# Expert layer of a transformer block: GpSimd left with transfers alone, weights written in sixteen pieces, selection in 16-bit one-hot form, list work in finer pieces

## The chip, the cores and the metric

One core of a Trainium2 chip runs the whole kernel in one launch. The metric is the time of an execution in microseconds on the device; the number for a kernel is the median of three runs.

## What is computed

One layer of a backbone for 512 latent and 256 context tokens of width 1024: a projection, a bidirectional mLSTM, grouped-query attention, a first layer norm, and then PEER, a layer that picks 128 of 16384 experts for every token. The change is in the last part:

```python
def _peer(h, wq, keys, u, v):          # P_BLOCK 128 tokens, 8 heads, 128 keys per half, top 16
    def block(xt):
        q = (xt @ wq).reshape(P_BLOCK, P_HEADS, 2, P_HALF)
        s = jnp.einsum('nhpd,hpkd->nhpk', q, keys)
        s1, i1 = lax.top_k(s[:, :, 0], P_TOPK)
        s2, i2 = lax.top_k(s[:, :, 1], P_TOPK)
        cand_s = (s1[..., :, None] + s2[..., None, :]).reshape(P_BLOCK, P_HEADS, P_TOPK * P_TOPK)
        cand_i = (i1[..., :, None] * N_KEYS + i2[..., None, :]).reshape(P_BLOCK, P_HEADS, P_TOPK * P_TOPK)
        top_s, pos = lax.top_k(cand_s, P_TOPK)
        idx = jnp.take_along_axis(cand_i, pos, axis=-1).reshape(P_BLOCK, P_HEADS * P_TOPK)
        g = jax.nn.softmax(top_s, axis=-1).reshape(P_BLOCK, P_HEADS * P_TOPK)
        act = jax.nn.gelu(jnp.einsum('nd,ned->ne', xt, u[idx]), approximate=False)
        return jnp.einsum('ne,ned->nd', g * act, v[idx])
```

and x = LN(alpha * x + gate2 * PEER(...)) behind it.

## The kernel before

The 512 tokens go in four tiles of 128. Each tile passes three stages.

**Selection** (`select`) is work of VectorE on a scratch that lies in the big tile `work` (128 x 16384 f32): top 16 of each of 16 score rows (L896 to L900), sums of candidates (L970, L973), top 16 of those. `weigh` then turns the positions into the two expert indices and a weight per pick, `iig`. For each half q, VectorE compares positions with 0 to 15 (is_equal, L952), GpSimd multiplies that one-hot tile by the indices (L954), and VectorE reduces (L962). The scores of tiles 1 to 3 come back from memory as `scfx` and `scfy`; those of tile 1 are read by GpSimd's queue.

**Lists** (`prelude`): transposes of `iig` (ptr, L991), then 16 units of 8 tokens. VectorE builds one-hot tiles A (L1008) and B (L1011), TensorE multiplies them into pf (which experts are used, and whether by one token) and pW (L1021), and ScalarE puts pW into `work` as the matrix of weights by expert and token. That matrix, Wd, 8.4 MB, goes to memory in four writes (L1028, SyncE's queue). `tables` and `look_up` (small steps that pass between TensorE, VectorE and ScalarE: pft, ppr, ppo, ppk) number the used experts and give two lists: `ri`, the expert of each of 29 x 128 rows, and `wi`, its row in Wd.

**Blocks** (`blocks`): 29 blocks of 128 experts per tile. GpSimd gathers uv (both matrices' rows, 1 MB) and wr (the weights, 64 KB) by the lists (L1108). In 12 of the 29 blocks every expert has one token: `token` finds it from wr on VectorE (jt, ti, L1147 and L1148), GpSimd gathers that token's row xg (512 KB), and VectorE takes the dot with u (L1168). In the other 17, TensorE transposes u (put, L1268; copied to ut by ScalarE, L1269) and multiplies by all tokens (s, L1282). Gelu on ScalarE (L1283), a multiply by wr on VectorE (L1284; for one-token blocks on ScalarE, L1185), and TensorE adds the block to py (L1196). `finish` adds the residual and does the second layer norm, two of its steps on GpSimd (L1255, L1258).

**Order.** A step of `blocks` issues for block i+5 the gathers (stage r of PIPE), for i+4 jt and ti (k), for i+3 the xg (u), for i+1 the dot (d), for i+2 the transposes (o), and so on to py of block i (a). The lists of tile t+1 are made while the blocks of tile t run: the driver (L1323 on) lets `select` and `prelude` go on by one step (one `yield`) whenever a table of costs (C_SEL, C_OH, ...; 43 steps and 131 units per tile) says so, at most to five blocks ahead of the tile's end (LATE). HEADS gives the steps of tile 0's selection and lists between which a step of the scores of tiles 2 and 3 is done (pwq, psc). `order_of` mixes the 12 one-token blocks into the 29. A scheduler then sets the order of each engine's instructions by dependences and the order in which the code issued them; each engine, and each DMA queue that it issues to, goes through them in order.

## Time and profile before

| | us |
|---|---|
| median of 3 runs | 1260.15 (1259.62 to 1260.58) |
| the profiled execution, its own time | 1269.07 |
| its span, first to last instruction | 1267.3 |
| TensorE (PE) busy in the span | 1051.4 (83%) |
| VectorE (DVE) busy | 850.2 (67%) |
| ScalarE (ACT) busy | 467.2 (37%) |
| GpSimd (POOL) busy | 523.0 (41%) |
| DMA, mean traffic | 284.16 MB at 224 GB/s |

The profile is of one execution. The blocks of the four tiles run from 589 us to the end. PE, DVE, ACT, POOL and SP are the five engines; PEld is TensorE loading weights, which runs beside its products. A DMA_INDIRECT of POOL of about 1 us is the issue of a gather, not its transfer. "<-" behind a wait names what ended last before the engine went on. PEclk is the clock that TensorE was granted, as a share of full speed.

### The profile page before, as it was taken

The page shows a single profiled execution, that of the slowest core. Times are in us where ns is not written, and L with a number is a line of the kernel's source. Part 1 is how long each engine was busy: PE and PEld are TensorE (multiplying, and loading weights), DVE is VectorE, ACT ScalarE, POOL GpSimd, SP SyncE. Part 2 cuts the span into 40 slices and gives each one's busy share as a digit, 9 for nine tenths or more (in the row PEclk, how much of TensorE's full clock was granted, in tenths as well). Part 3 has the DMA queues.
Part 4 walks back from the last instruction along what each step waited for, and adds up shares of the span by engine and source line. Part 5 has one row for each costly group of instructions (what it writes and reads, how often), then busy time and mean ns, then how long its engine had stood idle before and what let it go on. Part 6 is the DMA issues. An engine that isn't in the chain of part 4 may idle for free.

```text
span 1267.3 us, 19149 instructions
## 1 busy us (share of the span) xinstructions
PE 1051.4 (83%) x6784; PEld 844.8 (67%) x6784; DVE 850.2 (67%) x2655; ACT 467.2 (37%) x1132; POOL 523.0 (41%) x404
## 2 busy tenths in 40 slices
...
GB/s 364 222 200 227 140 134 35 116 41 3 1 151 216 226 264 191 60 91 344 247 255 248 253 364 187 153 293 307 345 410 227 216 291 323 414 314 302 326 350 120
DMA packets 102127, 284.16 MB, mean 224 GB/s; under 512 B 8548, under 2 KB 61512, under 8 KB 83976
## 3 DMA queue, kind: packets, MB, share of 16 engines
...
q8 instruction: 55, 0.90, 0.3%
...
## 4 chain that ended last, share of the span: by engine, by line
PE 45%; DVE 13%; DMA 9%; issue 5%; ACT 2%; POOL 2%; another core or an unknown queue 1%; DVEq 0%; ACTq 0%; POOLq 0%
PE py L1196 11%; PE pwq L838 8%; PE s L1282 6%; PE pW L1021 5%; DMA xg<-h2d,ti 5%; PE put L1268 2%; PE pf L1018 2%; DMA wr<-Wd,wi 2%; PE pw L769 2%; PE po L541 2%; DVE work L900 1%; PE ppt L567 1%; DVE work L897 1%; DVE work L898 1%; PE psc L846 1%
## 5 line engine op out<-in xcount | busy, mean ns | idle before, releaser
L1196 PE MATMUL py<-uv,wt 128*128 128x512 f32 x464 | 247.5, 654 | 25.1 <-DVE wt L1284 10.8
L1108 POOL DMA_INDIRECT uv<-in_uv,ri x116 | 120.8, 1041 | 131.9 <-PE py L1196 72.9
L1282 PEld LDWEIGHTS s<-ht,ut 128*128 128x128 f32 x1088 | 143.3, 205 | 40.6 <-ACT wt L1283 21.5
L1282 PE MATMUL s<-ht,ut 128*128 128x128 f32 x1088 | 152.5, 292 | 18.9 <-ACT wt L1283 17.9
L1108 POOL DMA_INDIRECT wr<-Wd,wi x116 | 121.2, 1045 | 54.8 <-issue 29.1
L1196 PEld LDWEIGHTS py<-uv,wt 128*128 128x128 f32 x464 | 84.4, 206 | 83.2 <-issue 54.8
L1269 ACT COPY ut<-put 128x512 f32<-128x512 f32 x136 | 75.3, 588 | 132.1 <-PE put L1268 85.1
L1021 PEld LDWEIGHTS <-A 128*128 128x128 f16 x1024 | 92.7, 147 | 23.1 <-issue 17.4
L1023 ACT ACTIVATE work<-pW 128x512 f32<-128x512 f32 x128 | 74.3, 597 | 89.7 <-PE pW L1021 64.8
L1021 PE MATMUL pW<-B,A 128*128 128x128 f16 x1024 | 98.0, 229 | 9.7 <-ACT work L1023 5.9
L1108 POOL DMA_INDIRECT xg<-h2d,ti x48 | 58.9, 1228 | 96.7 <-DVE ti L1148 44.9
L1268 PE MATMUL put<-cst,uv 128*128 128x128 f32 x544 | 79.4, 286 | 23.2 <-DMA uv<-in_uv,ri 14.4
L1268 PEld LDWEIGHTS put<-cst,uv 128*128 128x128 f32 x544 | 65.8, 149 | 47.3 <-issue 29.4
L838 PE MATMUL pwq<-h2T,wq 128*128 128x256 f32 x416 | 95.0, 380 | 0.0
L1168 DVE SCALAR_TENSOR_TENSOR xg<-xg,uv 128x1024 f32<-128x1024 f32 x48 | 58.6, 1220 | 49.7 <-DMA xg<-h2d,ti 49.7
L1018 PE MATMUL pf<-B,A 128*128 128x128 f16 x512 | 81.3, 230 | 10.5 <-DVE B L1011 10.5
L1011 DVE TENSOR_TENSOR B<-B,igr 128x1024 f16<-128x1024 f16 x128 | 83.3, 687 | 1.2
L838 PEld LDWEIGHTS pwq<-h2T,wq 128*128 128x128 f32 x416 | 76.8, 190 | 9.4 <-DMA wq<-in_wq 0.2
L1018 PEld LDWEIGHTS <-A 128*128 128x128 f16 x512 | 64.2, 148 | 22.2 <-issue 14.5
L1008 DVE TENSOR_TENSOR A<-iob,ig 128x1024 f16<-128x1024 f16 x64 | 46.5, 727 | 48.3 <-PE pW L1021 28.0
L208 POOL TENSOR_TENSOR wlo<-wi,whi 128x1024 fp32r<-128x1024 f32 (+1 forms) x18 | 48.5, 2711 | 59.9 <-ACT whi L207 59.8
L1284 DVE TENSOR_TENSOR wt<-wt,wr 128x128 f32<-128x128 f32 x68 | 25.7, 378 | 63.4 <-ACT wt L1283 52.9
...
## 6 DMA issues: line engine op xcount, KB each, us to landing
Wd<-work SPq DMA_DIRECT2D x16, 2048.0 KB, 22.1
...
wq<-in_wq SPq DMA_DIRECT2D x26, 512.0 KB, 4.9
...
wor<-in_w_out SPq DMA_DIRECT2D x8, 512.0 KB, 4.2
wql<-in_wq SPq DMA_DIRECT2D x6, 512.0 KB, 5.6
...
```

Of the source, the lines that this page charges most:

```text
L208: nc.gpsimd.tensor_tensor(lo[:, k:k + 4, 0:cw], wv[:, k:k + 4], hi[:, k:k + 4, 0:cw].bitcast(F32), op=ALU.subtract)
L838: nc.tensor.matmul(pt, w[:, k, :], h2T[:, k, t0 * P:(t0 + 2) * P], start=k == 0, stop=k == KC - 1)
L1011: nc.vector.tensor_tensor(B[:, q].rearrange("p a n r -> p a (n r)"), (B[:, 0] if q else ior).rearrange("p a n r -> p a (n r)"), igr[:, q, ...
L1018: nc.tensor.matmul(pf[:, 0:P], A[:, :, n], B[:, 0, :, n, :], start=c == 0 and n == 0, stop=c == P // TCH - 1 and n == TCH - 1)
L1021: nc.tensor.matmul(pw[:, (n - n4) * P:(n - n4 + 1) * P], A[:, :, n], B[:, q, :, n, :], start=q == 1, stop=q == 2)
L1023: nc.scalar.mul(Wn[:, :, n0 + n4:n0 + n4 + 4], pw.rearrange("p (n k) -> p k n", n=4), 1.0 / GSC)
L1108: nc.gpsimd.indirect_dma_start(out=dst, out_offset=None, in_=src, in_offset=bass.IndirectOffsetOnAxis(ap=ids, axis=0))
L1168: nc.vector.scalar_tensor_tensor(xg, xg, 1.0, w[:, 0:D], op0=ALU.mult, op1=ALU.mult, accum_out=nf)
L1196: nc.tensor.matmul(py[:, hs], wt, w[:, D + half * 512:D + half * 512 + 512], start=i == 0, stop=i == n - 1)
L1268: nc.tensor.transpose(pt[:, q * P:(q + 1) * P], w[:, (4 * kh + q) * P:(4 * kh + q + 1) * P], ident)
L1269: nc.scalar.copy(ut[:, 4 * kh:4 * kh + 4, :], pt.rearrange("p (q n) -> p q n", q=4))
L1282: nc.tensor.matmul(s_[:, 0:P], ut[:, k, :], ht[:, k, :], start=k == 0, stop=k == KC - 1)
```

## The change

In `weigh` the multiply and the cast move from GpSimd to VectorE, the one-hot tiles are f16 (a constant `place` holds 0 to 15), and four adds of halves replace each reduce. `finish` loads by SyncE's queue and replaces subtract-and-scale, multiply and add by two fused steps on VectorE. GpSimd then only issues transfers in the blocks. Wd goes out in 16 writes of 512 KB, one with each list step after the products (`send`; for tile 0 all 16 at once). The lists have 75 steps per tile, with three cuts per block (CUTS); unit c+1 of A and B is issued ahead of the products of unit c, and G of look_up likewise. jt comes one block earlier (k 5), xg one block earlier (u 4), and wr of a one-token block eight blocks ahead (ONE, an own set of 7 buffers). `order_of` starts the one-token blocks at .18 and spreads them over .76 for all tiles (before .15 and .7, for the last tile 0 and 1). HEADS has other places, and the costs sum to 147.

```diff
-C_SEL, C_OH, C_IIG, C_A, C_L, C_N = 5, 1.5, 6, 3.5, 1.5, 1
+C_SEL, C_OH, C_IIG, C_A, C_L, C_N, C_T = 1.7, 3, 2, 3.5, 1.5, 1, 1
+WPC = 16
-PIPE = (("r", 5), ("k", 4), ("u", 3), ("d", 1), ("o", 2), ("w", 1), ("h", 1), ("a", 0))
+PIPE = (("r", 5), ("k", 5), ("u", 4), ("d", 1), ("o", 2), ("w", 1), ("h", 1), ("a", 0))
+ONE = 8
+CUTS = "owa"
-HEADS = tuple(range(3, 35, 2))
-SPREAD = 0.7
-OFF = 0.5
+HEADS = (4, 8, 12, 15, 18, 21, 24, 28, 32, 38, 41, 44, 47, 50, 53, 58)
+SPREAD = 0.76
+FIRST = 0.18
@@ weigh
-            nc.gpsimd.tensor_copy(sif[:, hs].rearrange("p h q a -> p (h q) a"), si[:, 2 * h0:2 * (h0 + gh)])
+            nc.vector.tensor_copy(sih[:, hs].rearrange("p h q a -> p (h q) a"), si[:, 2 * h0:2 * (h0 + gh)])
...
-                    nc.vector.tensor_tensor(oh, abf[:, q, g0:g0 + n4].unsqueeze(3).to_broadcast([P, n4, 16, 16]),
-                                            iof[:, 0:16].unsqueeze(1).unsqueeze(1).to_broadcast([P, n4, 16, 16]), op=ALU.is_equal)
-                    eng.tensor_tensor(oh, oh, sif[:, h0 + g0:h0 + g0 + n4, q].unsqueeze(2).to_broadcast([P, n4, 16, 16]), op=ALU.mult)
-                    yield
+                nc.vector.tensor_tensor(oh, abh[:, q, 0:gh].unsqueeze(2).to_broadcast([P, gh, 16, 16]),
+                                        place.unsqueeze(1).to_broadcast([P, gh, 16, 16]), op=ALU.is_equal)
+                nc.vector.tensor_tensor(oh, oh, sih[:, hs, q].unsqueeze(3).to_broadcast([P, gh, 16, 16]), op=ALU.mult)
+                yield
+                for w in (8, 4, 2):
+                    nc.vector.tensor_tensor(oh[:, :, 0:w], oh[:, :, 0:w], oh[:, :, w:2 * w], op=ALU.add)
+                nc.vector.tensor_tensor(iig[:, q, ms].rearrange("p (h a) -> p h a", h=gh), oh[:, :, 0], oh[:, :, 1], op=ALU.add)
+                yield
...
-                nc.vector.tensor_reduce(iig[:, q, ms], oh, axis=AX.X, op=ALU.add)
@@ prelude
+    def send(n):
+        for _ in range(min(n, len(pieces))):
+            f, q = pieces.pop(0)
+            f(q)
...
+        AB = unit(0)
+        yield
+        for c in range(P // TCH):
+            last, AB = AB, unit(c + 1) if c + 1 < P // TCH else None
+            products(c, *last)
             yield
-        for q in range(4):
-            ks = slice(q * P // 4, (q + 1) * P // 4)
+        def rows_out(q):
+            ks = slice(q * P // WPC, (q + 1) * P // WPC)
             nc.sync.dma_start(Wd[t][0:NEXP, :].rearrange("(a k) n -> a k n", a=P)[:, ks], Wn[:, ks])
+        pieces.extend((rows_out, q) for q in range(WPC))
+        if t == 0:
+            send(WPC)
@@ order_of
-            return (b + 0.5) / n1 * spread + (1 - spread) * OFF if b < n1 else (b - n1 + 0.6) / (NBL - n1)
+            return (b + 0.5) / n1 * spread + FIRST if b < n1 else (b - n1 + 0.6) / (NBL - n1)
@@ blocks
+        for j, (t, i) in enumerate(items):
+            if seqs[t][i] < NB1[t]:
+                early.setdefault(max(j - ONE, t * n - LOOK), []).append((t, i))
...
-            wr = bp.tile([P, P], F32, tag="wr", name=f"wr{t}_{b}", bufs=LOOK + 2)
+            wr = bp.tile([P, P], F32, tag="wo" if one else "wr", name=f"wr{t}_{b}", bufs=ONE - 1 if one else LOOK + 1)
...
+            for e in early.get(i, ()):
+                weights_in(*e)
             for f, k in PIPE:
                 if 0 <= i + k < len(items):
                     stages[f](*items[i + k])
+                if f in CUTS[:-1]:
+                    yield
@@ finish
-        nc.gpsimd.dma_start(xt, x1d[ts_, :])
+        nc.sync.dma_start(xt, x1d[ts_, :])
...
-        layer_norm(pool, xt, f"l2_{t}")
-        yield
-        nc.gpsimd.tensor_tensor(xt, xt, y, op=ALU.mult)
...
-        nc.gpsimd.tensor_tensor(xt, xt, y, op=ALU.add)
+        mean, r = moments(pool, xt, f"l2_{t}")
...
+        nc.vector.scalar_tensor_tensor(xt, xt, mean, y, op0=ALU.subtract, op1=ALU.mult)
...
+        nc.vector.scalar_tensor_tensor(xt, xt, r, y, op0=ALU.mult, op1=ALU.add)
@@ the driver
-    cost = ([C_SEL] * 9 + [C_OH] * 4 + [C_IIG] + [C_A] * (P // TCH) + [C_N] + [C_L] * (NB1[1] // LB) + [C_N]
-            + [C_L] * -(-(NBL - NB1[1]) // LB) + [C_N])
+    cost = ([C_SEL] * 25 + [C_OH, 1.5] * 2 + [C_IIG, C_N, C_N] + [C_A] * (P // TCH + 1) + [C_N] + [C_T] * 5 + [C_N]
+            + [C_L] * (NB1[1] // LB + 1) + [C_T] * 5 + [C_N] + [C_L] * (-(-(NBL - NB1[1]) // LB) + 1) + [C_N])
...
-            g = i - START
+            g = i / len(CUTS) - START
...
                 if next(ahead, 0) is None:
+                    send(1)
```

Three places in the order of instructions. First VectorE, from the end of tile 0's lists on; ri and wi are the lists, jt, ti and wt belong to the first blocks, and the lines L896 to L904 are the selection of tile 1 with its scores scfx. Before, tile 1's selection was already under way when the lists ended, and at the first jt and wt its last heads stood in a row with them:

```order
L900 MAX_INDEX work<-work 128x8
L1147 SCALAR_TENSOR_TENSOR jt_0_5652,tk_0_5653<-wr_0_5633,iof 128x128
L898 MATCH_REPLACE work<-work,scfy_5628 128x128
L1148 TENSOR_SCALAR ti_0_5654<-tk_0_5653 128x1
L899 MAX work<-work 128x8 x2
L900 MAX_INDEX work<-work 128x8 x2
L970 TENSOR_TENSOR work<-work 128x64
L973 TENSOR_TENSOR work<-work 128x48
L896 MAX work<-work 128x8
L1284 TENSOR_TENSOR wt_12_5670<-wt_12_5670,wr_12_5617 128x128
L897 MAX_INDEX work<-work 128x8
```

Now the selection of tile 1 begins behind the first jt, ti and wt:

```order
L1145 SCALAR_TENSOR_TENSOR idf_5448<-kac_5449,idf_5448 128x29
L1146 CAST wi_5622<-idf_5448 128x29
L1147 TENSOR_SCALAR ri_5623<-idf_5448 128x29
L1204 SCALAR_TENSOR_TENSOR jt_0_5663,tk_0_5664<-wr_0_5639,iof 128x128
L1205 TENSOR_SCALAR ti_0_5665<-tk_0_5664 128x1
L1349 TENSOR_TENSOR wt_12_5700<-wt_12_5700,wr_12_5645 128x128
L900 MAX work<-scfx_5655 128x8 x2
L901 MAX_INDEX work<-work,scfx_5655 128x8
L902 MATCH_REPLACE work<-work,scfx_5655 128x128
L1349 TENSOR_TENSOR wt_13_5731<-wt_13_5731,wr_13_5649 128x128
```

So VectorE's queue holds the whole selection of tile 1 behind the multiply of the first block's weights (wt_12), where before that multiply stood among its last heads.

Second ScalarE, at the same place; ut are the copies of the transposes, wt the gelu of a block's products s, for the blocks 12, 13 and 14 that come first. Before:

```order
L1269 COPY ut_12_5635<-put_12_0_5636 128x512
L1269 COPY ut_12_5635<-put_12_1_5642 128x512
L1269 COPY ut_13_5657<-put_13_0_5658 128x512
L1269 COPY ut_13_5657<-put_13_1_5664 128x512
L1269 COPY ut_14_5688<-put_14_0_5689 128x512
L1269 COPY ut_14_5688<-put_14_1_5695 128x512
L1283 ACT_TABLE_LOAD
L1283 ACTIVATE wt_12_5670<-s_12_5671 128x128
L946 ACT_TABLE_LOAD
```

Now:

```order
L1334 COPY ut_12_5668<-put_12_0_5669 128x512
L1334 COPY ut_12_5668<-put_12_1_5675 128x512
L1334 COPY ut_13_5687<-put_13_0_5688 128x512
L1334 COPY ut_13_5687<-put_13_1_5694 128x512
L1348 ACT_TABLE_LOAD
L1348 ACTIVATE wt_12_5700<-s_12_5701 128x128
L1334 COPY ut_14_5718<-put_14_0_5719 128x512
L1334 COPY ut_14_5718<-put_14_1_5725 128x512
L1348 ACTIVATE wt_13_5731<-s_13_5732 128x128
```

The gelu of block 12 has moved ahead of the copies of block 14, and stands behind those of block 13 as before.

Third GpSimd, where the blocks of tile 1 begin; uv, wr and xg are gathers, L930 and L954 the cast and the multiplies for tile 2's selection. Before:

```order
L1248 DMA fx_7464<-x1d 128x1024
L930 CAST work<-work 128x256
L1108 DMA uv_1_7477<-in_uv,ri_7072 128x2048
L1108 DMA wr_1_7479<-Wd_3558,wi_7071 128x128
L1108 DMA xg_0_7481<-h2d,ti_0_7432 128x1024
L954 TENSOR_TENSOR work<-work 128x1024
L1108 DMA uv_16_7538<-in_uv,ri_7072 128x2048
L1108 DMA wr_16_7540<-Wd_3558,wi_7071 128x128
L954 TENSOR_TENSOR work<-work 128x1024 x3
L1108 DMA uv_2_7569<-in_uv,ri_7072 128x2048
L1108 DMA wr_2_7571<-Wd_3558,wi_7071 128x128
L1108 DMA xg_1_7573<-h2d,ti_1_7544 128x1024
```

Now:

```order
L1152 DMA wr_1_7430<-Wd_3558,wi_7122 128x128
L1152 DMA uv_0_7432<-in_uv,ri_7123 128x2048
L1152 DMA uv_15_7487<-in_uv,ri_7123 128x2048
L1152 DMA wr_15_7489<-Wd_3558,wi_7122 128x128
L1152 DMA xg_0_7491<-h2d,ti_0_7436 128x1024
L1152 DMA wr_2_7531<-Wd_3558,wi_7122 128x128
L1152 DMA uv_16_7533<-in_uv,ri_7123 128x2048
L1152 DMA wr_16_7535<-Wd_3558,wi_7122 128x128
L1152 DMA uv_1_7572<-in_uv,ri_7123 128x2048
L1152 DMA wr_3_7671<-Wd_3558,wi_7122 128x128
L1152 DMA uv_17_7673<-in_uv,ri_7123 128x2048
L1152 DMA wr_17_7675<-Wd_3558,wi_7122 128x128
```

The computing rows and the load of fx are gone from the queue, and wr_1, wr_2 and wr_3 of one-token blocks stand ahead of the uv of blocks 0, 1 and later.

## Rows read from the trace of the kernel before

**Rows 1.** Busy time by stage: the end of the list work of tile 0, the lead-in, and the blocks of the tiles 0, 1, 2 and 3. Columns: stretch, its length, then for PE, PEld, DVE, ACT and POOL the busy us with the number of instructions, the granted clock, the share of the DMA engines and GB/s.

```profile
510.00:589.00 79.00, 66.86 (x616) 60.18 (x614) 55.81 (x171) 42.87 (x118) 0.53 (x1) 0.93 0.37 141
589.00:618.00 29.00, 11.32 (x57) 10.22 (x58) 22.86 (x160) 6.26 (x9) 12.84 (x14) 0.67 0.69 258
618.00:798.00 180.00, 140.23 (x932) 100.13 (x932) 118.37 (x422) 62.45 (x173) 84.87 (x74) 0.88 0.71 261
798.00:970.00 172.00, 137.82 (x956) 99.55 (x954) 131.62 (x459) 71.28 (x181) 97.06 (x81) 0.90 0.82 301
970.00:1133.00 163.00, 131.00 (x934) 96.54 (x935) 91.44 (x235) 61.35 (x170) 91.12 (x79) 0.90 0.80 298
1133.00:1253.00 120.00, 103.53 (x502) 68.85 (x500) 30.82 (x88) 29.38 (x73) 64.64 (x60) 0.93 0.82 306
```

**Rows 2.** The tile py (sums of a token tile's blocks): its products, and its copy at a tile's end. Columns: count, shortest, median and longest ns, first and last start.

```profile
L1196 PE MATMUL py<-uv,wt x464: 592/592/1223, 617.8 to 1252.6; 128*128 128x512 f32 x155
L1201 ACT COPY y<-py x3: 994/1012/1013, 797.7 to 1133.8; 128x1024 f32<-128x1024 f32 x3
```

**Rows 3.** The chain of waits from 589 to 1253, by line.

```profile
by line: PE py L1196 20.5%; PE s L1282 10.8%; DMA xg<-h2d,ti 9.7%; issue 8.5%; PE pW L1021 7.7%; PE put L1268 4.7%; DMA wr<-Wd,wi 4.4%; PE pf L1018 3.4%; DVE work L900 2.3%; DVE work L898 2.1%; DVE work L897 2.1%; another core or an unknown
```

**Rows 4.** Busy time of shorter stretches, with the columns of rows 1.

```profile
720.00:760.00 40.00, 18.20 (x111) 12.32 (x110) 9.04 (x42) 10.31 (x39) 8.22 (x8) 0.77 0.88 346
800.00:840.00 40.00, 27.16 (x126) 17.11 (x125) 37.10 (x61) 11.16 (x21) 29.75 (x18) 0.74 0.55 189
900.00:940.00 40.00, 27.20 (x151) 17.47 (x149) 18.00 (x108) 18.83 (x72) 14.93 (x16) 0.87 1.00 404
940.00:980.00 40.00, 34.36 (x191) 25.25 (x190) 39.72 (x203) 13.97 (x33) 22.50 (x20) 0.91 0.71 261
980.00:1000.00 20.00, 9.27 (x46) 5.72 (x44) 11.57 (x24) 4.24 (x9) 14.38 (x9) 0.85 0.44 162
1080.00:1100.00 20.00, 6.54 (x27) 3.39 (x25) 3.92 (x21) 3.79 (x14) 3.77 (x4) 0.66 1.01 421
```

**Rows 5.** VectorE's timeline, single instructions: the first and the last of tile 1's selection (L896, L945), two jt (L1147) and a dot (L1168). Columns: start, duration, operation, and in brackets the idle time before it and what ended that.

```profile
579.84 0.48 DVE L896 MAX8 work<-scfx 128x8 f32<-128x128 f32 x2
...
615.46 0.27 DVE L1147 SCALAR_TENSOR_TENSOR jt<-wr,iof 128x128 f32<-128x128 f32 x1
...
618.82 0.27 DVE L945 TENSOR_TENSOR work<-work 128x128 f32<-128x128 f32 x1
...
653.72 8.05 DVE L1147 SCALAR_TENSOR_TENSOR jt<-wr,iof 128x128 f32<-128x128 f32 x1 [2.19 <-DMA wr<-Wd,wi]
...
735.29 1.22 DVE L1168 SCALAR_TENSOR_TENSOR xg<-xg,uv 128x1024 f32<-128x1024 f32 x1 [12.27 <-DMA xg<-h2d,ti]
```

**Rows 6.** GpSimd's timeline: the first gather of xg, and the four multiplies of tile 1's selection.

```profile
616.33 0.94 POOL L1108 DMA_INDIRECT xg<-h2d,ti  x1 [12.48 <-DVE work L899]
...
652.35 9.26 POOL L954 TENSOR_TENSOR work<-work 128x1024 f32<-128x1024 f32 x4
```

**Rows 7.** TensorE's waits from 589 to 1253, those for the tables. Columns: who waited for whom, us in total, times, longest.

```profile
PE ppr L1053 <- DVE Fw L1050: 18.6, 2, 13.4
...
PE ppr L1054 <- DVE Fw L1051: 14.8, 2, 10.0
...
PE ppk L1075 <- DVE Fw L1072: 11.8, 1, 11.8
```

**Rows 8.** Groups of instructions from 589 to 1253, shapes apart. Columns: line, engine, operation, out<-in, shapes, count, busy us, mean ns of one, idle time before them.

```profile
L1011 DVE TENSOR_TENSOR B<-B,igr 128x1024 f16<-128x1024 f16 x96 | 62.7, 687 | 0.8
...
L1168 DVE SCALAR_TENSOR_TENSOR xg<-xg,uv 128x1024 f32<-128x1024 f32 x48 | 58.6, 1220 | 49.7 <-DMA xg<-h2d,ti 49.7
...
L954 POOL TENSOR_TENSOR work<-work 128x1024 f32<-128x1024 f32 x12 | 30.4, 2551 | 4.5 <-DVE work L952 2.1 <-DVE rtl L97 1.2 <-DVE rtl L100 1.2
...
L952 DVE TENSOR_TENSOR work<-work,iof 128x1024 f32<-128x1024 f32 x12 | 19.5, 1624 | 0.0
...
L962 DVE TENSOR_REDUCE iig<-work 128x128 f32<-128x2048 f32 x6 | 13.6, 2278 | 6.9 <-POOL work L954 6.9
...
L1255 POOL TENSOR_TENSOR fx<-fx,y 128x1024 f32<-128x1024 f32 x3 | 7.8, 2590 | 16.1 <-DMA y<-in_ln_g 13.0 <-DVE fx L745 3.1
...
L1258 POOL TENSOR_TENSOR fx<-fx,y 128x1024 f32<-128x1024 f32 x3 | 7.1, 2357 | 0.2
...
L745 DVE TENSOR_SCALAR fx<-fx,lmvl,rrl 128x1024 f32<-128x1024 f32 x3 | 2.4, 812 | 0.1
```

**Rows 9.** ScalarE's timeline at the first blocks of tile 0: copies of ut, a table load and the first gelu.

```profile
606.11 1.07 ACT L1269 COPY ut<-put 128x512 f32<-128x512 f32 x2 [8.61 <-remote]
...
609.35 1.28 ACT L1283 ACT_TABLE_LOAD   x1
610.64 0.28 ACT L1283 ACTIVATE wt<-s 128x128 f32<-128x128 f32 x1
```

**Rows 10.** DMA issues of the page: writes of Wd, and loads of 512 KB. Columns: queue, count, KB of each, median us to landing.

```profile
Wd<-work SPq DMA_DIRECT2D x16, 2048.0 KB, 22.1
...
wq<-in_wq SPq DMA_DIRECT2D x26, 512.0 KB, 4.9
```

**Rows 11.** VectorE's waits from 589 to 1253, those for gathered data.

```profile
DVE jt L1147 <- DMA wr<-Wd,wi: 53.0, 15, 8.7
...
DVE xg L1168 <- DMA xg<-h2d,ti: 49.7, 13, 12.3
```

More of the change, by code (lines that the diff above doesn't have):

```diff
@@ L880, in tile_block @@
     pcol = sel.tile([P, 1], F32, name="pcol")
+    place = sel.tile([P, 16, 16], F16, name="place")
     identb = sel.tile([P, P], F16, name="identb")
@@ L959, in weigh @@
                                     den[:, hs].unsqueeze(2).to_broadcast([P, gh, 16]), op=ALU.mult)
-            for q in range(2):
-                oh = scr[:, 4096 * q if t else 4096 + 1024 * q:][:, 0:256 * gh].rearrange("p (m b) -> p m b", b=16)
-                nc.vector.tensor_reduce(iig[:, q, ms], oh, axis=AX.X, op=ALU.add)
             yield
@@ L979, in select @@
                 yield from weigh(h + 1 - gh)
+    pieces = []
+    def send(n):
+        for _ in range(min(n, len(pieces))):
+            f, q = pieces.pop(0)
+            f(q)
     def prelude(t):
@@ L1001, in prelude, with unit @@
             nc.scalar.copy(igr[:, q], ig[:, 1 + q].unsqueeze(2).to_broadcast([P, P, RUN]))
+        yield
         pf = bank(f"pf{t}", "pf")
-        for c in range(P // TCH):
-            n0 = c * TCH
-            ns = slice(n0, n0 + TCH)
+        def unit(c):
+            ns = slice(c * TCH, (c + 1) * TCH)
             A = tl([P, P, TCH], F16, f"A{c}_", "A", 2)
@@ L1014, in prelude, with products @@
                                             [P, P // RUN, TCH * RUN]), op=ALU.mult if q else ALU.is_equal)
+            return A, B
+        def products(c, A, B):
             for n4 in range(0, TCH, 4):
@@ L1054, in tables @@
             nc.tensor.matmul(pr[:, P:2 * P], dF, trinb, start=True, stop=True)
+            yield
             nc.vector.tensor_copy(cs, pr[:, P - 1:P])
+            nc.scalar.copy(T[:, 0:P], pr[:, P:2 * P])
+            yield
             po = bank(f"ppo{t}_{i}", "p")
@@ L1068, in look_up, with reach @@
             nc.vector.tensor_scalar(of, jls, -1.0, off, op0=ALU.mult, op1=ALU.add)
-            for j in range(0, b1 - b0, LB):
+            js = range(0, b1 - b0, LB)
+            def reach(j):
                 k = min(LB, b1 - b0 - j)
```

53 lines of the change are left out of this document (36 added, 17 removed).

## Prediction, made before the changed kernel was run

> **What bounds the kernel now.** I read the stages first. The first 589 us of the span are everything up to the lists of token tile 0; TensorE is busy nearly all the time at their end [rows 1], and the change touches little there. The other 664 us are the 4 x 29 blocks: TensorE is busy for 11.3 + 140.2 + 137.8 + 131.0 + 103.5 = 523.9 us of them and idle for 140, VectorE is busy for 395 [rows 1]. No engine is full over a whole tile, so a tile's length is set by who waits for whom. The first product of py starts at 617.8; the tiles end where py is copied out, the first at 797.7, the third at 1133.8 [rows 2]. The chain of waits from 589 on agrees: py a fifth, and behind TensorE's own lines the gather of xg with 9.7% and of wr with 4.4%, 64 and 29 us [rows 3].
>
> Then stretches of 20 and 40 us, to see where TensorE's 140 us are lost. Around each tile's Wd write it does 18.2 of 40 (720 to 760), 27.2 of 40 (900 to 940) and 6.54 of 20 (1080 to 1100), with DMA at .88 to 1.01: lost are 21.8, 12.8 and 13.5 us, together 48 [rows 4]. At a tile's first blocks, where the next tile's selection ends and finish runs, it does 27.2 of 40 (800 to 840) and 9.27 of 20 (980 to 1000): 12.8 and 10.7 lost [rows 4]. Third, the lead-in: TensorE does 11 of 29 us there [rows 1], while VectorE runs tile 1's selection (39.0 us, 579.84 to 618.82) with the first block's jt behind it until 615.46 [rows 5], and GpSimd stands before the xg for 12.48 us [rows 6]. Last, TensorE waits 18.6 + 14.8 + 11.8 us for steps of the tables on VectorE [rows 7]; in tile 0's Wd window they stand there behind a dot that waits 12.27 us for its xg [rows 5].
>
> **GpSimd only transfers.** Before, the four one-hot multiplies hold GpSimd for 30.4 / 3 = 10.1 us per tile, and finish's two for 2.59 + 2.36 = 4.9 [rows 8]; every gather of the next blocks stands behind them. Once they also hold VectorE: a jt, 0.27 us elsewhere, takes 8.05 us while GpSimd runs the four multiplies from 652.35 to 661.61 [rows 5, 6]. VectorE now gets the work. Per tile it loses four is_equal of 1.62 and two reduces of 2.28, 11.1 us [rows 8]. It gains, for each of two q, one is_equal and one multiply of 2048 f16 and adds of 1024, 512, 256 and 128. By the f16 row (0.687 for 1024) that is 1.37 + 1.37 + 0.69 and, halved on with a floor near 0.2 us, an estimated 0.8 for the other three: 4.2. If the multiply with its repeated operand goes no faster than the reduce over 2048 (2.28), a q costs 5.1. So 8.4 to 10.2 against 11.1; I take 1.5 us less per tile. Finish adds two scalar_tensor_tensor of 1.22, near the dot's row, and drops one tensor_scalar of 0.81 [rows 8]: +1.6. VectorE's load hardly moves, and GpSimd's queue is rid of 15 us per tile.
>
> The multiply is where a rule can be set against a row. The B products, all f16, take 0.687 us for 1024 [rows 8]. The Trainium skill (VectorE: DVE Perf Modes, "What auto-detection actually checks") says that the doubled rate for 16-bit data needs every tensor to have step 1 or -1; the multiply's sih operand is repeated innermost, so by it the multiply stays at the slow end, 0.9 us per q more than the f16 row, 1.8 per tile. No row of this trace has such an operand.
>
> **The lead-in.** In the new order VectorE does jt_0, ti_0 and wt_12 right after the lists, ahead of the selection, and the read of tile 1's scores stands in GpSimd's queue behind the first gathers. So the selection can no longer start at 580: it stands behind wt_12, which needs the gelu of the first block. ScalarE had a hold of its own there: the copy of the second block's ut waited 8.61 us, until 606.11, for something that no row names, and the gelu came at 610.64, after the copies of that block and of the next and a table load of 1.28 [rows 9]. In the new order that block's copies are still ahead of the gelu, the next one's no longer are: gelu near 608.5, first py near 609 at the earliest. One more step of the later tiles' scores now stands ahead of tile 0's tables; TensorE is 66.86 of 79 us busy there [rows 1], which bounds it to 0 to 6 us, and what the ScalarE copy waits for hides most of it. I take first py at 609 against 617.8.
>
> The price is that all 39 us of selection, 38 of which lay ahead of the first py, now lie in tile 0's blocks: VectorE has 118.4 + 39.0 + 2 = 160 us to do there [rows 1, 5]. At a share of 1.0 the tile ends at 769; at the .765 of the next tile (131.6 of 172, the densest stage [rows 1]) at 818. From 940 to 980 it did 39.7 of 40 [rows 4], so it can be full. I take .92, between the two and nearer to full, since it waits for less (xg earlier, no GpSimd in its way): end at 783, **-14**. The break-even is 160 / (798 - 609) = .85.
>
> **Finer steps and paced writes.** The list work is the same in 75 steps a tile instead of 43, cut three times a block; no row prices a cut, and I give it nothing beyond the share above. The 8.4 MB of Wd went out as 4 writes in one step, 22.1 us to land [rows 10]. Now 16 writes ride on 16 steps; by the driver's costs these are about 17 of 147 units, of which it spends 147 / 18 per block in tile 0 and 147 / 29 later: 2.1 and 3.4 blocks, 12 and 20 us. The most that any window moved is 421 GB/s [rows 4]; 8.4 MB in 20 us is just that, so pacing by itself gives little. What helps is the lead: xg is asked for a block (172 / 29 = 5.9 us) earlier, and wr of a one-token block three blocks earlier. VectorE waited 53.0 us for wr in jt and 49.7 for xg in the dot [rows 11]; a block takes 5.9 off a wait of 12, so I give each of the two later windows 6 of its 13 us.
>
> A size rule speaks against the small writes. A write of 2 MB, four in flight, landed in 22.1 us, and a load of 512 KB in 4.9 [rows 10]. The Trainium skill (DMA: Bandwidth & Descriptors, "Measured (HBM→SBUF, 128 partitions, SWDGE, issued from GpSimd)") says to batch to at least 1 MiB for 75% of peak; the pieces are half of that. What it would do here is the fourth rival.
>
> **Sum.** Tile 0: -14. Tile 1: 8 of the 12.8 us at its first blocks (of GpSimd's 10 us ahead of the gathers), 6 of its Wd window, 4 of the tables' waits: -18. Tile 2: 6 of 10.7, 6 of 13.5, 2: -14. Tile 3 has no list work; it is idle for 120 - 103.5 = 16.5 us [rows 1], half of it given to the leads: -8. Together -54: span 1213.3, with the 1.8 us around it 1215.1. The profiled execution was 1269.07 against a median of 1260.15; taking the same 8.9 off gives **1206**.
>
> **Rivals.** *VectorE takes the gain* (1237): its queue is in order, and each finer step stands between a block's jt, dot and wt. At a share of .86 tile 0 ends at 795, -3, and the others keep half, -20. For it: VectorE is full at 940 [rows 4]; against it: over the 664 us it is idle for 269. *Pacing doesn't pace* (1228): the 48 us of the Wd windows stay, since 12 to 20 us is as fast as writes can go; left are -4, -12, -8 and -8. For it: the rates above; against it: the longer lead of xg. *The lost head start decides* (slower, 1280): VectorE goes no denser than .765 in tile 0, which ends at 818, +20, and as the same queue sets the pace later, nothing comes back. It decides below .85. For it: no tile had more than .77; against it: those stages had GpSimd's stalls in them. *Small pieces go one after another* (slower, 1284): 16 x 4.9 = 78 us instead of 22, so the next tile's wr are there at block 28 and not 24, some 26 us late, three times: +78 less the 54. Against it: the four writes before overlapped.
>
> **How the numbers follow.** Forecast .55 (own range 1184 to 1226), below that .05, VectorE takes the gain .15, no pacing .12, lost head start .10, pieces in a row .03. The range 1172 to 1248 leaves out the two slow ones (.13), the upper tail of the VectorE case (.04) and a little below. 0.2%, some 2.5 us, is about what a measurement of this kernel can tell from no change; .03 of the first four comes out within it. So faster .84, same .03, slower .13.
>
> **What would show it.** First py near 609, not 618; py of tile 0 copied out near 783 with VectorE at about .92 between; no jt of 8 us; GpSimd busy with transfers alone; TensorE above 14 of 20 us in the later Wd windows; waits for wr in jt well below 53 us. An end of tile 0 past 798, or the last Wd piece of a tile more than 30 us behind the first, would make it wrong.

## Result and the profile after

The changed kernel took 1209.97 us (1209.55 to 1213.08, 4 runs) against 1260.37 us of the kernel before in the same comparison: 0.9604 of it, 95% interval 0.9585 to 0.9622. Its profiled execution took 1209.55 us, so profile against profile the gain is 59.5 us, between the medians 50.4: the profiled execution before lay 8.7 us above its median.

Busy time by stage of the changed kernel, the lead-in and the four tiles, with the columns of [rows 1]:

```profile
589.00:607.00 18.00, 9.41 (x57) 9.05 (x58) 1.68 (x10) 4.97 (x8) 12.73 (x14) 0.59 0.86 308
607.00:790.30 183.30, 144.39 (x937) 99.64 (x935) 144.34 (x646) 66.06 (x177) 77.34 (x74) 0.89 0.79 282
790.30:941.40 151.10, 132.93 (x945) 97.18 (x946) 119.01 (x456) 65.19 (x177) 76.80 (x71) 0.95 0.89 335
941.40:1090.60 149.20, 131.38 (x953) 95.99 (x952) 81.60 (x232) 62.81 (x173) 78.88 (x72) 0.95 0.88 338
1090.60:1194.00 103.40, 95.01 (x492) 62.99 (x490) 30.10 (x92) 27.75 (x71) 54.64 (x55) 1.00 0.88 339
```

and the tile py:

```profile
L1253 PE MATMUL py<-uv,wt x464: 592/592/1219, 607.0 to 1193.4; 128*128 128x512 f32 x155
L1258 ACT COPY y<-py x3: 1007/1013/1015, 790.3 to 1090.6; 128x1024 f32<-128x1024 f32 x3
```

Against [rows 1, 2]: the first py comes at 607.0 instead of 617.8. Tile 0 is no shorter (183.3 for 180), the next three are: 151.1 for 169.5, 149.2 for 166.6, 103.4 for 119.5. TensorE's idle time in them is 38.9, 18.2, 17.8 and 8.4 us; before it was 39.8, 31 (its tile 1 ended at 967.2), 35 and 16.5. The rest is busy time: in the last tile nearly the same products (one block's eight transposes, about 1 us, now fall ahead of it) take 95.0 instead of 102.9 us, at a granted clock of 1.00 instead of .93.

VectorE at the lists' end (ri) and the first blocks, as in [rows 5]:

```profile
588.69 0.17 DVE L1147 TENSOR_SCALAR ri<-idf 128x29 int32<-128x29 f32 x1
...
602.21 0.32 DVE L1204 SCALAR_TENSOR_TENSOR jt<-wr,iof 128x128 f32<-128x128 f32 x1 [13.35 <-DMA wr<-Wd,wi]
...
604.80 0.29 DVE L1349 TENSOR_TENSOR wt<-wt,wr 128x128 f32<-128x128 f32 x1 [2.08 <-issue]
605.01 0.48 DVE L900 MAX8 work<-scfx 128x8 f32<-128x128 f32 x2
```

VectorE now stands still from 588.9 to 602.2, for the wr of the first block, and begins tile 1's selection at 605.0 instead of 579.8. In the lead-in it works for 1.7 of 18 us. ScalarE's hold of 8.61 us ahead of the second block's copy [rows 9] has no counterpart: that block's copies come by 602.0 and the first gelu at 604.5; a hold of 4.75 us that no row names now stands ahead of the second gelu, at 610.8.

Forty microseconds of the changed kernel from the first Wd write of the tiles 1, 2 and 3 on, the same columns:

```profile
716.00:756.00 40.00, 28.98 (x147) 18.59 (x146) 18.92 (x120) 17.82 (x74) 8.53 (x10) 0.83 0.99 390
863.00:903.00 40.00, 32.36 (x163) 20.08 (x162) 18.48 (x113) 17.71 (x70) 12.27 (x12) 0.87 1.01 405
1016.00:1056.00 40.00, 32.99 (x182) 21.43 (x182) 12.95 (x72) 18.19 (x73) 13.55 (x15) 0.91 1.01 404
```

TensorE does 94.3 of 120 us. Before, it was 18.2 and 27.2 of 40 in the first two [rows 4] and 25.0 in 40 us from 1069 on, together 70.4:

```profile
1069.00:1109.00 40.00, 24.96 (x138) 15.74 (x138) 12.46 (x65) 17.51 (x70) 15.77 (x16) 0.83 1.01 413
```

VectorE's waits for gathered data from 589 to the end, beside [rows 11]:

```profile
DVE xg L1225 <- DMA xg<-h2d,ti: 46.6, 12, 9.0
...
DVE jt L1204 <- DMA wr<-Wd,wi: 15.1, 2, 13.3
```

The wait of jt for wr has gone from 53.0 to 15.1 us, 13.3 of it in the lead-in. That of the dot for xg is almost what it was (49.7).

VectorE's groups, shapes apart, beside [rows 8]:

```profile
L1349 DVE TENSOR_TENSOR wt<-wt,wr 128x128 f32<-128x128 f32 x68 | 19.6, 288 | 102.8 <-ACT wt L1348 79.1 <-issue 23.5
...
L957 DVE TENSOR_TENSOR work<-work 128x2048 f16<-128x2048 f16 x6 | 13.7, 2284 | 0.0
L1204 DVE SCALAR_TENSOR_TENSOR jt<-wr,iof 128x128 f32<-128x128 f32 x48 | 13.6, 284 | 15.1 <-DMA wr<-Wd,wi 15.1
...
L955 DVE TENSOR_TENSOR work<-work,place 128x2048 f16<-128x2048 f16 x6 | 7.3, 1218 | 0.0
```

The one-hot multiply (L957) takes 2.28 us, the is_equal of the same size 1.22. The multiply by wr (L1349, formerly L1284) took 0.378 us on average before.

### The profile page after: what moved, and what is told of

Read it like the earlier page. It is cut to its first block, busy times and chain, and to the rows that moved or that the text cites. A ratio compares the mean times of both kernels' runs of the same rounds, so it can differ in the third digit from the quotient of the medians.

```text
span 1207.8 us, 19196 instructions
## 1 busy us (share of the span) xinstructions
PE 1039.1 (86%) x6784; PEld 833.3 (69%) x6784; DVE 821.1 (68%) x2698; ACT 464.1 (38%) x1132; POOL 460.6 (38%) x374
## 4 chain that ended last, share of the span: by engine, by line
PE 42%; DVE 14%; DMA 10%; issue 4%; ACT 3%; another core or an unknown queue 2%; POOL 1%; SPq 0%; DVEq 0%; ACTq 0%; POOLq 0%
PE py L1253 9%; PE pwq L841 9%; PE pW L1040 5%; DMA xg<-h2d,ti 5%; PE s L1347 5%; PE pw L772 2%; PE pf L1037 2%; PE put L1333 2%; DMA Wd<-work 2%; PE po L544 2%; DVE xg L1225 1%; DVE work L904 1%; PE psc L849 1%; DVE work L902 1%
## 5 line engine op out<-in xcount | busy, mean ns | idle before, releaser
L1253 PE MATMUL py<-uv,wt 128*128 128x512 f32 x464 | 241.0, 641 | 27.6 <-DVE wt L1349 16.4
L1152 POOL DMA_INDIRECT uv<-in_uv,ri x116 | 123.6, 1066 | 337.1 <-DMA scd<-sc 158.0
L1347 PE MATMUL s<-ht,ut 128*128 128x128 f32 x1088 | 143.9, 282 | 9.0 <-issue 5.7
L1347 PEld LDWEIGHTS s<-ht,ut 128*128 128x128 f32 x1088 | 133.7, 196 | 23.6 <-issue 16.9
L1040 PEld LDWEIGHTS <-A 128*128 128x128 f16 x1024 | 89.1, 147 | 25.4 <-issue 15.2
L1040 PE MATMUL pW<-B,A 128*128 128x128 f16 x1024 | 94.7, 227 | 11.7 <-ACT work L1043 7.0
L1333 PE MATMUL put<-cst,uv 128*128 128x128 f32 x544 | 82.8, 292 | 18.5 <-DMA uv<-in_uv,ri 11.3
L1349 DVE TENSOR_TENSOR wt<-wt,wr 128x128 f32<-128x128 f32 x68 | 19.6, 288 | 102.8 <-ACT wt L1348 79.1
L1037 PE MATMUL pf<-B,A 128*128 128x128 f16 x512 | 70.8, 227 | 0.0
L1037 PEld LDWEIGHTS <-A 128*128 128x128 f16 x512 | 57.6, 147 | 11.7 <-issue 9.5
L1152 POOL DMA_INDIRECT xg<-h2d,ti x48 | 50.3, 1048 | 40.3 <-DVE idf L1122 11.0
```

The lines of the kernel that those rows point to most:

```text
L1037: nc.tensor.matmul(pf[:, 0:P], A[:, :, n], B[:, 0, :, n, :], start=c == 0 and n == 0, stop=c == P // TCH - 1 and n == TCH - 1)
L1040: nc.tensor.matmul(pw[:, (n - n4) * P:(n - n4 + 1) * P], A[:, :, n], B[:, q, :, n, :], start=q == 1, stop=q == 2)
L1152: nc.gpsimd.indirect_dma_start(out=dst, out_offset=None, in_=src, in_offset=bass.IndirectOffsetOnAxis(ap=ids, axis=0))
L1253: nc.tensor.matmul(py[:, hs], wt, w[:, D + half * 512:D + half * 512 + 512], start=i == 0, stop=i == n - 1)
L1333: nc.tensor.transpose(pt[:, q * P:(q + 1) * P], w[:, (4 * kh + q) * P:(4 * kh + q + 1) * P], ident)
L1347: nc.tensor.matmul(s_[:, 0:P], ut[:, k, :], ht[:, k, :], start=k == 0, stop=k == KC - 1)
```

## The experiments

Twelve kernels ran, on two chips. There the kernel before takes 1232.6 to 1235.3 us, 2% less than in the first comparison, and so does the changed kernel: its ratio came out as 0.9604 again. So ratios to the kernel before are compared (1% is 12.3 us), and traces, but for a few rows of the changed kernel above, only among these runs. Lengths of the tiles in us:

| run | ratio (interval) | tile 0 | 1 | 2 | 3 |
|---|---|---|---|---|---|
| r5_after | 0.9604 (0.9566 to 0.9641) | 165.2 | 149.7 | 140.5 | 101.9 |
| e1_wd4 | 0.9667 (0.9627 to 0.9706) | 164.0 | 156.3 | 144.8 | 101.8 |
| e2_lead | 0.9692 (0.9653 to 0.9731) | 167.0 | 152.8 | 140.7 | 110.0 |
| e12_lead_wd4 | 0.9749 (0.9711 to 0.9788) | 165.3 | 156.6 | 144.3 | 107.5 |
| e4_pool | 0.9949 (0.9916 to 0.9982) | 179.7 | 165.0 | 146.2 | 115.0 |
| e6_pool_weigh | 0.9875 (0.9840 to 0.9909) | 179.0 | 160.4 | 144.4 | 112.1 |
| e7_pool_finish | 0.9712 (0.9662 to 0.9763) | 165.9 | 158.0 | 140.5 | 113.0 |
| e8_before_pool | 0.9769 (0.9733 to 0.9805) | 148.2 | 169.0 | 150.6 | 112.5 |
| e9_no_cuts | 0.9719 (0.9692 to 0.9745) | 158.3 | 169.8 | 146.3 | 105.1 |
| e10_last_tile | 0.9692 (0.9669 to 0.9716) | 168.5 | 151.2 | 139.1 | 115.4 |
| e3_scores_act | 0.9453 (0.9414 to 0.9491) | 147.0 | 150.6 | 140.2 | 103.1 |
| e11_repeat | 0.9427 (0.9393 to 0.9461) | 150.9 | 143.2 | 139.7 | 102.9 |

**r5_after**, the changed kernel itself.

> The changed kernel again, on the chip on which the next three run (the four runs above were on another chip than the first comparison, where the kernel before takes 1235 us and not 1260, so their ratios to it are not yet to be set against 0.960). Ratio 0.955 to 0.965 by all theories; if it is lower, leads and pieces were worth more than the ratios 0.969 and 0.967 seem to say.

0.9604: the reference for the rest.

**e1_wd4** and **e2_lead**, the pieces and the leads of jt and xg undone (wr still comes eight blocks ahead), and **e12_lead_wd4** with both:

```diff
-WPC = 16
+WPC = 4
-PIPE = (("r", 5), ("k", 5), ("u", 4), ("d", 1), ("o", 2), ("w", 1), ("h", 1), ("a", 0))
+PIPE = (("r", 5), ("k", 4), ("u", 3), ("d", 1), ("o", 2), ("w", 1), ("h", 1), ("a", 0))
```

> The changed kernel (1210.0 us), with Wd written in 4 pieces of 2 MB instead of 16 of 512 KB, still one with each list step. In its trace SyncE issues the 16 pieces of a tile without a pause, in 25 to 31 us, whatever list step they stand in. Theory (the longer leads of xg and wr carried the Wd windows, the pieces nothing): 1206 to 1214, and TensorE as busy in the Wd windows as with 16 pieces. Rival (16 pieces let the gathers through, 4 crowd them out): 15 to 30 us slower, 1225 to 1240, with waits of the dots for xg of 12 us again.

> The changed kernel with the old leads, jt four and xg three blocks ahead of py; all else stays. Theory (the leads carried the Wd windows and tile 3): 15 to 25 us slower, 1225 to 1235, most of it in the Wd windows and 5 in tile 3. Rival (leads are worth little since xg is asked for when it can be): 1208 to 1214.

> The changed kernel with the old leads of jt and xg and with Wd in 4 pieces, both undone at once; alone they cost 0.9 and 0.65% of the kernel before. Theory (each takes its own share of the Wd windows): the sum, 0.973 to 0.979. Rival (each alone covers for the other): 0.985 and more, with TensorE in the Wd windows back at 8 to 10 of 20 us.

e1 lost 0.6% (8 us) and e2 0.9% (11 us); both lie between what the theory and the rival had put on them. Forty microseconds from the first Wd write on, r5_after and then e1_wd4:

```profile
703.00:743.00 40.00, 29.73 (x167) 19.53 (x166) 22.50 (x146) 19.61 (x78) 10.32 (x11) 0.91 1.01 406
843.00:883.00 40.00, 30.73 (x160) 19.67 (x159) 18.27 (x112) 15.90 (x64) 10.32 (x11) 0.87 1.01 407
988.00:1028.00 40.00, 29.14 (x162) 18.74 (x161) 13.08 (x72) 17.41 (x69) 14.39 (x15) 0.91 1.02 405
```

```profile
703.00:743.00 40.00, 29.79 (x161) 19.64 (x159) 19.42 (x125) 18.94 (x77) 9.60 (x12) 0.87 1.01 413
844.00:884.00 40.00, 25.02 (x123) 15.39 (x122) 12.81 (x70) 10.90 (x42) 10.39 (x10) 0.83 1.00 410
993.00:1033.00 40.00, 24.00 (x128) 15.19 (x128) 11.60 (x61) 11.40 (x45) 11.27 (x12) 0.83 1.01 410
```

TensorE does 89.6 us in the three stretches with 16 pieces, 78.8 with 4 (11 us less); with the old leads 86.1. The longest wait of a dot for its xg in these stretches is 7.4, 8.6 and 9.4 us with 16 pieces, and 8.5, 12.7 and 15.7 with 4. So of the two it is the pieces that carried most of the Wd windows, though not by the pacing of list steps. SyncE comes to a tile's 16 writes one straight after the other (the row of 30.64 us below), and what holds it between them are its own earlier writes. Its waits for landed pieces in the changed kernel, in us in total, times and longest:

```profile
SPq L1054 <- DMA Wd<-work: 45.6, 18, 5.0
```

e2's loss is mostly in the last tile, 8 of its 11 us. Both undone cost 1.45%, the sum within its interval: each has its own share, and neither covers for the other.

**e4_pool**, GpSimd computing again, and its two halves **e6_pool_weigh** and **e7_pool_finish**; **e8_before_pool** is the reverse, the kernel before with that part alone:

```diff
-                nc.vector.tensor_tensor(oh, oh, sih[:, hs, q].unsqueeze(3).to_broadcast([P, gh, 16, 16]), op=ALU.mult)
+                    eng.tensor_tensor(oh, oh, sif[:, h0 + g0:h0 + g0 + n4, q].unsqueeze(2).to_broadcast([P, n4, 16, 16]), op=ALU.mult)
...
-        nc.vector.scalar_tensor_tensor(xt, xt, mean, y, op0=ALU.subtract, op1=ALU.mult)
+        nc.gpsimd.tensor_tensor(xt, xt, y, op=ALU.mult)
...
-        nc.vector.scalar_tensor_tensor(xt, xt, r, y, op0=ALU.mult, op1=ALU.add)
+        nc.gpsimd.tensor_tensor(xt, xt, y, op=ALU.add)
```

> The changed kernel with GpSimd computing again: cast and four f32 one-hot multiplies per tile and finish's multiply and add on GpSimd, reduces on VectorE, loads of finish on the queues of before. Theory (GpSimd's 15 us per tile stood ahead of the gathers at each tile's first blocks): 12 to 20 us slower, 1222 to 1230, lost in the first 45 us of tiles 1 and 2 and at the end of tile 1's selection in tile 0. Rival (the one-hot multiply of 2.28 us now on VectorE costs as much as it saves): 1206 to 1213.

> The changed kernel with only the selection's cast and one-hot multiplies back on GpSimd in f32, finish as in the changed kernel. With both parts back the time was 3.5% above the changed kernel's ratio, much more than the 12 to 20 us expected. Theory (the selection's 10 us per tile, twice finish's, stand ahead of the gathers): two thirds of the loss, 2 to 2.6% slower than the changed kernel. Rival (it is VectorE that loses, where GpSimd works at the same time, and finish is the longer overlap with block work): under 1.2%.

> The changed kernel with only finish's multiply and add back on GpSimd, with the loads of finish on the queues of before. Theory (5 us of GpSimd per tile and waits for the loads of ln_g on its queue): 0.8 to 1.5% slower than the changed kernel. Rival (finish is what cost most, since GpSimd waits there for the load of ln_g with all gathers behind it): 2% and more.

> The kernel before with only the GpSimd part of the change (f16 one-hot on VectorE, finish on VectorE, its loads on SyncE's queue); order, leads, pieces and list steps stay as they were. Theory (the GpSimd part is most of the gain, and stands by itself): 0.965 to 0.975 of the kernel before. Rival (it pays only together with the finer steps, since VectorE's multiplies otherwise sit in one lump): 0.985 to 1.00.

Undone, the part costs 3.45% (42 us, more than twice the expectation): the selection 2.7%, finish 1.1%. Alone, on the kernel before, it brings 2.3% (28 us), more than half of the whole gain, a little less than the theory had. GpSimd's timeline at the end of tile 1's selection in e6_pool_weigh, then VectorE's over the same microseconds:

```profile
642.66 6.67 POOL L958 TENSOR_TENSOR work<-work 128x1024 f32<-128x1024 f32 x2 [3.23 <-DVE work L956]
650.49 5.60 POOL L958 TENSOR_TENSOR work<-work 128x1024 f32<-128x1024 f32 x2 [1.16 <-DVE work L956]
656.24 1.08 POOL L1154 DMA_INDIRECT wr<-Wd,wi  x1
```

```profile
643.77 3.36 DVE L1227 SCALAR_TENSOR_TENSOR xg<-xg,uv 128x1024 f32<-128x1024 f32 x1
...
647.06 4.49 DVE L956 TENSOR_TENSOR work<-work,iof 128x1024 f32<-128x1024 f32 x2
651.47 0.27 DVE L962 TENSOR_REDUCE den<-work 128x8 f32<-128x128 f32 x1
651.67 2.22 DVE L1351 TENSOR_TENSOR wt<-wt,wr 128x128 f32<-128x128 f32 x1
...
653.93 2.31 DVE L1206 SCALAR_TENSOR_TENSOR jt<-wr,iof 128x128 f32<-128x128 f32 x1
```

No gather is issued until 656.24. And VectorE is slow in the same stretch: a dot takes 3.36 us (1.22 elsewhere), the next two is_equal 4.49 together (2.4), a multiply by wr 2.22 (0.29), a jt 2.31 (0.28). So for the selection both readings of the expectations hold at once; how its 33 us divide between the two is not shown. For finish only one does: in e7_pool_finish the means of VectorE's instructions stay as in r5_after (multiply by wr 0.287, jt 0.284, dot 1.22 us), and what is seen is GpSimd standing in finish, 13.9 us for VectorE and 8.0 for the load of ln_g, with the gathers of the next blocks behind it.

**e3_scores_act**: the scores of the last two tiles leave by ScalarE's queue.

```diff
     def to_memory(t, j, src):
...
-        nc.sync.dma_start(scd[t:t + 2, :, j * P:(j + 1) * P].rearrange("t p n -> p t n"), sc_)
+        nc.scalar.dma_start(scd[t:t + 2, :, j * P:(j + 1) * P].rearrange("t p n -> p t n"), sc_)
```

> The changed kernel with the last tiles' scores written by ScalarE's queue instead of SyncE's, where the last two stand 18.45 us behind the 16 Wd pieces of tile 0. Gathers and the read of tile 1's scores wait for these writes. With that the read comes early and the selection of tile 1 stands ahead of tile 0's first jt on VectorE again, as before the change. Theory (VectorE's 26 idle us between lists and first blocks are what tile 0 lacks): 8 to 15 us faster, 1195 to 1202, tile 0's end from 790 to 776 to 782. Rival (first py goes back to 617 since jt and wt stand behind the selection): 1208 to 1216.

1.5% (18.6 us) faster, more than expected, all in tile 0 (165.2 to 147.0); first py at 606.9. What moved is the read of tile 1's scores (scfx) in GpSimd's queue, and with it the selection on VectorE. The read in r5_after, then the read and the selection's first row in e3_scores_act:

```profile
597.50 0.60 POOL L1286 DMA_DIRECT2D scfx<-scd  x1
```

```profile
460.29 0.74 POOL L1286 DMA_DIRECT2D scfx<-scd  x1 [29.20 <-DMA wql<-in_wq]
...
582.10 0.48 DVE L900 MAX8 work<-scfx 128x8 f32<-128x128 f32 x2
```

In r5_after the read stands behind seven gathers. The theory put that down to SyncE's queue. SyncE's timeline in the kernel before, in the changed kernel, and in e1_wd4 with its read and selection; column two goes from the start of a row's first issue to the end of its last:

```profile
568.21 2.85 SPq L1028 DMA_DIRECT2D Wd<-work  x3
572.74 1.73 SPq L864 DMA_DIRECT2D scd<-sc  x2
```

```profile
566.54 18.45 SPq L1054 DMA_DIRECT2D Wd<-work  x16
585.09 2.42 SPq L867 DMA_DIRECT2D scd<-sc  x2
...
715.93 30.64 SPq L1054 DMA_DIRECT2D Wd<-work  x16
```

```profile
566.40 3.07 SPq L1054 DMA_DIRECT2D Wd<-work  x4
570.52 1.68 SPq L867 DMA_DIRECT2D scd<-sc  x2
...
598.25 0.60 POOL L1286 DMA_DIRECT2D scfx<-scd  x1
...
604.20 0.49 DVE L900 MAX8 work<-scfx 128x8 f32<-128x128 f32 x2
```

The 16 pieces of tile 0 hold SyncE's queue for 18.45 us and the last two score writes go out at 585.09 instead of 572.74. But with 4 pieces they go out at 570.52, and yet the read stands where it stood, the selection begins at 604.20 (604.12 in r5_after), and tile 0 takes 164.0 us (165.2). So the 16 issues are not what delays the selection. (With 4 pieces the score writes need 18.8 us to land, so they land no earlier. In the kernel before they needed 16.4, and there the read went out at 496.2.) The gathers hardly lose by these writes, though the profile of the changed kernel puts the wait of the first uv down to them: that uv is issued 0.9 us behind the list ri in the changed kernel and in e1_wd4, 0.3 us behind it in e3_scores_act. And in e3_scores_act the read goes out 111 us ahead of the last score write (571.19), so there it doesn't need the space that these writes free. What e3 shows is what the early read is worth. Why the order of instructions has it so late in the changed kernel is not shown; in e8_before_pool these writes are SyncE's too, and the read goes out at 461.9.

With the early read the selection is early again; the lead-in and tile 0, r5_after and then e3_scores_act:

```profile
589.00:606.10 17.10, 9.82 (x57) 9.46 (x58) 1.71 (x10) 4.97 (x8) 12.63 (x14) 0.58 0.88 325
606.10:771.30 165.20, 134.33 (x933) 94.89 (x932) 142.28 (x646) 66.24 (x176) 78.27 (x74) 0.95 0.84 311
```

```profile
589.00:607.00 18.00, 9.67 (x57) 8.94 (x58) 18.00 (x131) 4.96 (x8) 12.65 (x14) 0.65 0.95 360
607.00:754.00 147.00, 127.76 (x935) 93.98 (x935) 118.64 (x487) 67.53 (x177) 77.08 (x72) 0.97 0.88 331
```

VectorE fills the lead-in (18.0 of 18 us) and has 118.6 instead of 142 us left to do in tile 0.

**e9_no_cuts** and **e10_last_tile**:

```diff
-CUTS = "owa"
+CUTS = "a"
-    seqs = [order_of(NB1[t], SPREAD) for t in range(NT)]
+    seqs = [order_of(NB1[t], SPREAD) for t in range(NT - 1)] + [
+        sorted(range(NBL), key=lambda b: (b + 0.5) / NB1[3] if b < NB1[3] else (b - NB1[3] + 0.6) / (NBL - NB1[3]))]
```

> The changed kernel (0.9604 of the kernel before on two chips) with one cut per block instead of three; list steps stay as fine and keep their costs, but several follow each other in the code at a block's end. Theory (GpSimd part, leads and pieces carry 3.8 of the 4.0%, the finer mixing about nothing): 0.956 to 0.965. Rival (with cuts the list work fills TensorE's and VectorE's gaps): 0.97 and more.

> The changed kernel with the order of the last tile's blocks as before (one-token blocks spread over all 29). The last tile went from 119.5 to 103 us, twice the 8 us predicted. Theory (half of it is idle time that the leads took away, half products at the full granted clock): 0.958 to 0.964, last tile 102 to 107. Rival (the block order did it): 0.967 to 0.972, last tile 110 to 114.

Both rivals had the time right. Without cuts the kernel is 1.15% slower: tile 1 loses 20 us (TensorE is idle there for 34 us instead of 17), tile 2 6 and tile 3 3, tile 0 gains 7. With the old order the last tile takes 13.5 us more. The last tile in r5_after and in e10_last_tile:

```profile
1061.50:1163.40 101.90, 94.75 (x492) 63.08 (x490) 30.12 (x93) 27.36 (x71) 53.28 (x55) 1.00 0.89 352
```

```profile
1063.00:1178.60 115.60, 101.92 (x501) 66.27 (x499) 29.43 (x86) 28.62 (x73) 55.82 (x57) 0.94 0.86 326
```

Of the 13.7 us, 6.5 are idle time and 7 are busy time, about 1 of it a block's transposes that fall into the tile, the rest the same products at a lower granted clock.

**e11_repeat**: on top of e3, ScalarE writes the indices out 16 times, so that no operand of the multiply is repeated.

```diff
-                nc.vector.tensor_tensor(oh, oh, sih[:, hs, q].unsqueeze(3).to_broadcast([P, gh, 16, 16]), op=ALU.mult)
+                rp = scr[:, 9216 + 1024 * q:9216 + 1024 * q + 128 * gh].bitcast(F16).rearrange(
+                    "p (h b a) -> p h b a", h=gh, b=16)
+                nc.scalar.copy(rp, sih[:, hs, q].unsqueeze(3).to_broadcast([P, gh, 16, 16]))
+                nc.vector.tensor_tensor(oh, oh, rp, op=ALU.mult)
```

> The changed kernel with the scores written by ScalarE's queue (0.9453) and, beyond it, the indices repeated 16 times by ScalarE ahead, so that the one-hot multiply of VectorE reads all operands with step 1. Theory (the repeated operand keeps the multiply at one element a step): the multiply goes from 2.28 to 1.2 to 1.4 us, and the time by 2 to 5 us, 0.941 to 0.944. Rival (the multiply is slow for its size or place, not for the repeated operand): 2.28 us stays, time 0.945 to 0.948.

The copy and the multiply, mean ns behind the bar:

```profile
L959 ACT COPY work<-work 128x2048 f16<-128x2048 f16 x6 | 11.3, 1893 | 5.5 <-DVE work L933 5.5
...
L960 DVE TENSOR_TENSOR work<-work 128x2048 f16<-128x2048 f16 x6 | 7.3, 1213 | 0.0
```

The multiply takes 1.21 us instead of 2.28, as the theory had it. The time, 1162.2 us, is the lowest of all, but its interval overlaps e3's: what the repeat is worth beyond e3 is not settled. Both versions beat the changed kernel.

## Why the prediction came out right

1206 was forecast and 1210 measured, but profile against profile it was -54 against -59.5, and the tiles were -14, -18, -14 and -8 against -7.4 (with the lead-in), -18.4, -17.4 and -16.1. The 8.9 us that the sum took off for the profiled execution of before had no counterpart after (1209.55 against a median of 1209.97). Point by point:

- **Lead-in.** Right in the order and in the time: the selection begins right behind wt_12, first py at 607.0 for 609, lists at the same time as before. What set that time was not as forecast: the gelu came at 604.5, not 608.5, and py then stood behind the 16 products s of the next block on TensorE until 607. The bound of 0 to 6 us for the extra scores step was nothing.
- **Tile 0.** The end at 783 was 790.3. Two terms failed here and partly cancelled. VectorE's work was 144 us, not 160: the 39.0 was elapsed time with steps of the lists in it, and the 118.4 held instructions drawn out by GpSimd (one jt alone by 7.8 us), which the sum carried over. Its share was .79, not .92. The lost head start had a price that the prediction didn't see. It read the new order and took it as given; e3 shows that with the read of tile 1's scores early, tile 0 is 18 us shorter. The rival "lost head start decides" was near in the share (.765 for .79) and had the work too high; the rest of the change paid for it.
- **GpSimd only transfers.** The mis-sized term. The sum took 8 + 6 us for it, from queue time of 15 us per tile, and for VectorE nothing but a part of tile 0's share. Undone it costs 42 us and alone it brings 28. The one row of 8.05 us in [rows 5, 6] was read as a single event; it was a second mechanism: groups of the kernel before have the same lengthening in their means (wt .378 for .288, jt .449 for .284).
- **The one-hot multiply.** The sum took 1.5 us less work per tile; at the slow end, 2.28, a q costs 1.22 + 2.28 + 0.69 + 0.42 + 0.28 + 0.29 = 5.2 and a tile 10.4 against 11.1. The Trainium skill (VectorE: DVE Perf Modes, "What auto-detection actually checks") asks step 1 or -1 of every tensor for the doubled rate; the trace agrees, 2.28 with the repeated operand and 1.21 without (e11). Of 1.8 us per tile so decided the total shows nothing.
- **Wd windows.** The 6 us each were about right (5.2 and 8.0 for tiles 1 and 2, 10.8 for tile 0), the reason was not. The prediction gave them to the leads and held that pacing by itself gives little; e1 shows that 16 pieces are worth 8 us, and e2 that the leads of jt and xg give less in these windows. What paces the pieces is SyncE's wait for earlier pieces to land, so that it takes 25 to 31 us for 16, where 4 take 3; the list steps have no part in it. One sign of being wrong was met by this, barely: the last piece of a tile more than 30 us behind the first (30.3 us in tile 0's window, 24.7 in the next two). The loss that it stood for did not come.
- **Tile 3.** Idle time fell by 8.2 us, as forecast. The other 8 are nearly all the products at a higher granted clock, for which the sum had no term. Leads, selection, finish and block order are each needed for this tile: undoing any one (e2, e6, e7, e10) gives back 8 to 13.5 us.
- **Finer steps.** Given nothing; e9 shows 14 us for the cuts.

So three terms were too small (GpSimd, the clock of tile 3, the cuts), and what made the sum come out is the 18 us of tile 0 that the change itself lost. That it came within 4 us is luck; that GpSimd's freed queue, denser Wd windows and less idle time in tile 3 would each give time was right.

The pieces undone one by one (GpSimd 42, cuts 14, leads and pieces 18, last order 11 us) add up to 85, not to 49, nor to the 67 that 49 would be without the late selection. The GpSimd part is worth 42 us in company and 28 alone. So each part pays more while the others keep the blocks dense, and single costs of this kind can't be added.

Not settled: why the read of tile 1's scores stands late in the changed kernel, how the selection's loss on GpSimd divides between held gathers and slow VectorE, what ScalarE's holds in the first blocks wait for, and why both kernels took 2% less in these runs than in the first comparison. HEADS and the earlier wr of one-token blocks (ONE) were not tried by themselves. The wait of jt for wr is gone in every run that has ONE (12.8 us in e2_lead) and not in e8_before_pool (45.5), which lacks it along with the other parts.
